# Projecting the small columns (decay, beta, forget gate) ahead of q, k and v in a hybrid mixer layer

## Chip, cores and metric

The kernel runs on one core of one Trainium2 chip. The metric is the device time of one execution in microseconds. The median of three runs of the kernel before is 900.4 us (899.67 to 903.23).

## What is computed

One transformer layer for a sequence of 512 tokens with 1024 channels, all in float32. The input is normalised to `h`, multiplied by one wide matrix `w_in`, and its columns feed four branches of 256 channels: a gated delta rule over chunks of 64 tokens, a latent attention, a gated linear attention and an attention with a forget gate. The branches are merged with sigmoid gates, and an MLP follows. The part that matters here is the delta rule's input and the rows of small columns:

```python
qkv = silu(causal_depthwise_conv(dn_qkv, dn_conv))          # 768 columns, 4 taps
a_q, a_k = l2_normalize(a_q), l2_normalize(a_k)             # per head of 64
beta = sigmoid(dn_b)                                        # 4 columns
g = -exp(dn_a_log) * softplus(dn_a + dn_dt_bias)            # 4 columns, cumsum per chunk
log_f = log_sigmoid(fox_f + fox_f_bias)                     # 4 columns, cumsum over the sequence
```

The sums of `g` become the decay factors of the delta rule, and the sums of `log_f` enter the logits of the forget-gate attention.

## The kernel before

**Matmuls.** Every float32 operand of a projection is split into a high part (a cast on ACT, L155) and a low part (a subtraction on DVE, L156), and a product is three matmuls (`mm3`, L250). `proj` (L254) computes 128 columns of a projection for all 512 tokens: 8 blocks of the 1024 channels, three matmuls each, 24 in all, into one accumulator in PSUM. The accumulators (`acc`) have two buffers.

**Weights.** `raw_cols` (L223) loads 128 columns of weights with a DMA on SP's queue into one of four raw buffers. `w_split` (L229) splits them into a pair of buffers, of which there are three.

**Order of the work.** The code is written in the order of the computation, and the framework then lays down one fixed queue per engine before the run, by the place in the program and by its own estimate of when inputs are ready. So later work fills gaps in earlier work, and an engine's queue need not follow the lines.

**Around the change.** After the input is normalised and the value columns of two branches are projected (L360 to L369), the loop of L396 projects q, k and v of the delta rule in six tiles of 128 columns (two each). For each tile DVE reads the accumulator four times (L399 and three times L402: the four taps of the convolution), `silu` (L371) takes three ACT steps and one DVE multiplication (L377), and the q and k tiles are squared, split and summed per head with matmuls (`sumsq`, L205, its matmuls L210 and L211) into `ps_n`. That is issued two tiles late, for m from 2 to 5.

Then comes a seventh tile, the small columns (`w_misc`, L413 and L414), whose columns the host has gathered. Rows 96 to 107 hold the forget gate, the decay and beta. DVE adds the bias (L420), ACT copies the other rows (L422), and POOL issues a load of a mask (L424). `softplus` (L379 to L392) is three ACT steps and seven DVE operations on 32 partitions. DVE scales (L429), scans along the tokens into RF (L430), clears a part (L431) and subtracts from the chunk's last sum (L433).

The tile RF then also gets the norms, in rows 0 to 31: a logarithm on ACT of `ps_n` (L436) and a DVE operation (L437). RS holds RF in two parts (L439 to L442). Matmuls with RF (L447) and RS (L456, L467) spread the rows for the decay matrices (`decay_pair`, L463); their results, times the products of keys and queries (L481, L485), go into the triangular solve. The projections of the gates and of the other branches (L529 to L580) fill TensorE meanwhile. Two DMAs per head on SP's queue (L546, L547) copy rows of RF for the forget-gate attention.

Temporaries (`tmp`) have four buffers; `softplus` takes three of them, `silu` one, `sumsq` three.

Of the kernel before, what the change touches and what calls it, by code (L numbers as in the profile page):

```python
# [12 lines left out]
ALU = mybir.AluOpType  # L13
# [3 lines left out]
P = 128  # L17
D = 1024
S = 512
# [17 lines left out]
DN_Q, DN_Z, DN_B, DN_A = 0, 768, 1024, 1028  # L37
# [16 lines left out]
V_CONV, V_PRE, V_MLP, V_BG, V_QN, V_KN, V_GB, V_DN, V_GN = 0, 24, 32, 40, 72, 74, 75, 76, 77  # L54
# [66 lines left out]
def hybrid_mixer_kernel(ctx, tc, I, out):  # L121
    nc = tc.nc
    pe, dve, act, pool, sp = nc.tensor, nc.vector, nc.scalar, nc.gpsimd, nc.sync
# [13 lines left out]
    def ps_acc():  # L137
        return psp.tile([P, 512], F32, name="acc", tag="acc", bufs=2)
# [3 lines left out]
    def ps_sm(*tags):  # L142
        tags = tags or banks["ring"]
        banks["i"] += 1
        t = tags[banks["i"] % len(tags)]
        return psp.tile([P, 512], F32, name=t, tag=t, bufs=1)
# [7 lines left out]
    def split(hi, lo, src, eng=dve):  # L154
        act.copy(out=hi, in_=src)  # L155
        eng.tensor_tensor(out=lo, in0=src, in1=hi.bitcast(F32), op=ALU.subtract)  # L156
# [37 lines left out]
    indz = const.tile([P, 134], F32R, name="indz")  # L194
# [10 lines left out]
    def sumsq(ps, lhsT, src, t, first, last):  # L205

        sq, hi, lo = t("sq"), t("sqh", F32R), t("sql", F32R)
        act.activation(out=sq, in_=src, func=AF.Square)
        split(hi, lo, sq)
        pe.matmul(out=ps, lhsT=lhsT, rhs=hi, start=first, stop=False)  # L210
        pe.matmul(out=ps, lhsT=lhsT, rhs=lo, start=False, stop=last)  # L211

    vec = lambda r: vecs[:, r:r + 1]
# [4 lines left out]
    w_in = I["w_in"][0]  # L218
# [4 lines left out]
    def raw_cols(w, c0):  # L223

        rv = raw_tile().rearrange("p (k c) -> p k c", k=KD)
        sp.dma_start(out=rv, in_=w.rearrange("(k p) c -> p k c", p=P)[:, :, c0:c0 + P])
        return rv

    def w_split(rv, where=None, eng=dve):  # L229
        wp, wb, tag = where or (wpool, 3, "w")  # L230
        hi = wp.tile([P, 1024], F32R, name="whi", tag=tag + "hi", bufs=wb)
        lo = wp.tile([P, 1024], F32R, name="wlo", tag=tag + "lo", bufs=wb)
        shape = rv.shape
        n = 1
        for d in shape[1:]:
            n *= d
        if len(shape) == 3:
            hv = hi[:, 0:n].rearrange("p (k c) -> p k c", k=shape[1])
            lv = lo[:, 0:n].rearrange("p (k c) -> p k c", k=shape[1])
        else:  # L240
            hv, lv = hi[:, 0:n], lo[:, 0:n]
        split(hv, lv, rv, eng)
        return hv, lv

    def stat_tiles(w, c0, ncol):

        for c in range(c0, c0 + ncol, P):
            yield w_split(raw_cols(w, c))
# [5 lines left out]
    def proj(wt, rh, rl, sl=slice(0, S), ps=None, clear=True):  # L254
        ps = ps_acc() if ps is None else ps
        hi, lo = wt
        for k in range(KD):
            mm3(ps[:, sl], hi[:, k], lo[:, k], rh[:, k, sl], rl[:, k, sl], clear and k == 0, k == KD - 1)
        return ps


    hh = big_tile("hh", F32R)
    hl = big_tile("hl", F32R)
# [81 lines left out]
    def slot(name, tag, bufs, dt=F32):  # L345
        return br.tile([P, S], dt, name=name, tag=tag, bufs=bufs)
# [14 lines left out]
    for g in range(2):  # L361
        ws = gv_w if g == 0 else [w_split(rows_4k(X_V, a)) for a in range(2)]
        for t in range(NT):
            ps = ps_acc()
# [6 lines left out]
    def silu(dst, src):  # L371

        sg = tmp("sg")
        act.activation(out=sg, in_=src, func=AF.Exp, scale=-1.0)
        act.activation(out=sg, in_=sg, func=AF.Ln, bias=1.0)
        act.activation(out=sg, in_=sg, func=AF.Exp, scale=-1.0)
        dve.tensor_tensor(out=dst, in0=src, in1=sg, op=ALU.mult)  # L377
# [14 lines left out]
        dve.scalar_tensor_tensor(out=dst, in0=z, scalar=0.0, in1=l, op0=ALU.max, op1=ALU.add)  # L392


    qkvT = []
    for m, wt in enumerate(stat_tiles(w_in, DN_Q, 768)):  # L396
        ps = proj(wt, hh, hl)
        y = slot("qkvT", "qkvT", 6)
        dve.tensor_scalar(out=y, in0=ps, scalar1=vec(V_CONV + 18 + m), scalar2=None, op0=ALU.mult)  # L399
        for j in range(3):  # L400
            sh = 3 - j
            dve.scalar_tensor_tensor(out=y[:, sh:], in0=ps[:, 0:S - sh], scalar=vec(V_CONV + 6 * j + m),  # L402
                                     in1=y[:, sh:], op0=ALU.mult, op1=ALU.add)
        silu(y, y)
        qkvT.append(y)
        if 2 <= m < 6:
            n_ = m - 2
            if n_ == 0:
                ps_n = ps_sm()
            sumsq(ps_n, indz[:, 6 - 2 * n_:6 - 2 * n_ + P], qkvT[n_], tmp, n_ == 0, n_ == 3)  # L410


    mraw = raw_cols(I["w_misc"], 0)  # L413
    misc = proj(w_split(mraw), hh, hl)  # L414
# [6 lines left out]
                      scalar2=cst[R9, _CO["rowc"][0]:_CO["rowc"][0] + 1], op0=ALU.add, op1=ALU.mult)  # L421
# [10 lines left out]
    gch = RF[R9].rearrange("p (n c) -> p n c", c=C)  # L432
    dve.tensor_tensor(out=RF[32:64].rearrange("p (n c) -> p n c", c=C),  # L433
                      in0=gch[:, :, C - 1:C].broadcast_to([32, NCH, C]), in1=gch, op=ALU.subtract)
    ps = ps_n
    act.activation(out=RF[0:32], in_=ps[0:32], func=AF.Ln, bias=eps_col[0:32])  # L436
    dve.tensor_scalar(out=RF[0:32], in0=RF[0:32], scalar1=-0.5,  # L437
                      scalar2=cst[0:32, _CO["rowc"][0] + 1:_CO["rowc"][0] + 2], op0=ALU.mult, op1=ALU.add)
# [6 lines left out]
    ps = ps_sm()  # L445
# [8 lines left out]
    ps = ps_sm()  # L454
# [52 lines left out]
    for p in range(2):  # L507
        ps = ps_sm()
# [8 lines left out]
    for src, outs in ((kbg, ((kbg, 4), (ktl, 12))), (vb, ((vb, 8),))):  # L517
        for p in range(2):
            ps = ps_sm()
            for j in range(NT):  # L520
                pe.transpose(out=ps[:, j * P:(j + 1) * P], in_=src[p][:, j * P:(j + 1) * P], identity=ident)
            for lst, c0 in outs:
                dve.tensor_tensor(
                    out=lst[p].rearrange("p (j e c) -> p j e c", j=NT, e=2),
                    in0=ps.rearrange("p (j e c) -> p j e c", j=NT, e=2),
                    in1=cols[:, :, c0 + 2 * p:c0 + 2 * p + 2].unsqueeze(3).broadcast_to([P, NT, 2, C]),
# [21 lines left out]
    for p in range(2):  # L548
        for c0, dst, sc in ((X_Q, fq, 0.125), (X_K, fk, 1.0)):
            ps = proj(w_split(raw_cols(w_in, c0 + P * p)), hh, hl)  # L550
# [3 lines left out]
    for wt in stat_tiles(w_in, G_Q, 256):  # L554
        ps = proj(wt, hh, hl)
# [3 lines left out]
    for wt in stat_tiles(w_in, M_CQ, 384):  # L559
        ps = proj(wt, hh, hl)  # L560
# [35 lines left out]
    for c in range(31, 0, -1):  # L596
# [4 lines left out]
                          in1=z0[:, c:c + 1, l_:16].broadcast_to([P, c, w_]), op=ALU.mult)  # L601
# [12 lines left out]
    for z in (1, 0):  # L614
        (pool, dve)[z].tensor_tensor(out=XD[z].rearrange("p g (b c) -> p g b c", c=32),
                           in0=XC[z].unsqueeze(2).broadcast_to([P, H * NT, 2, 32]),
                           in1=cv("blk2").unsqueeze(1).unsqueeze(3).broadcast_to([P, H * NT, 2, 32]), op=ALU.mult)
# [25 lines left out]
    for h in range(H):  # L643
        y = AT[h]
# [3 lines left out]
        ps = ps_sm()  # L648
# [7 lines left out]
        ps = ps_sm()  # L656
# [23 lines left out]
    for n in range(NCH):  # L680
        j, o = n // 2, n % 2
# [15 lines left out]
        if n < NCH - 1:  # L697
# [4 lines left out]
            for e in range(2):  # L702
                es = slice(C * e, C * e + C)
                for p in range(2):
                    dve.scalar_tensor_tensor(out=nxt[es, p, es], in0=cur[es, p, es], scalar=cd[es, p, n:n + 1],
                                             in1=psk[es, p * P + C * e:p * P + C * e + C], op0=ALU.mult, op1=ALU.add)
# [35 lines left out]
    ps = ps_sm()  # L742
# [5 lines left out]
    for n in range(NCH):  # L748
        cs = slice(C * n, C * n + C)
        dve.tensor_tensor_scan(out=gB[:, cs], data0=onesr.bitcast(F32)[:, 0:C], data1=gz[:, cs], initial=0.0,  # L750
                               op0=ALU.mult, op1=ALU.add)
# [9 lines left out]
                      in1=gBv[:, :, C - 1:C].broadcast_to([P, NCH, C]), op=ALU.subtract)  # L761
# [6 lines left out]
    ps = ps_sm()  # L768
# [58 lines left out]
    for h in range(H):  # L827
# [3 lines left out]
        ps = ps_sm()  # L831
# [13 lines left out]
    for n in range(NCH):  # L845
        j, o = n // 2, n % 2
# [8 lines left out]
        if n > 0:  # L855
            sm_ = gp.tile([P, 256], F32, name="Smask", tag="Smask", bufs=2)
            dve.tensor_tensor(out=sm_.rearrange("p (h c) -> p h c", c=C), in0=cur.unsqueeze(1).broadcast_to([P, H, C]),
                              in1=cv("bd32").rearrange("p (h c) -> p h c", c=C), op=ALU.mult)
# [3 lines left out]
        if n < NCH - 1:  # L862
# [7 lines left out]
            else:  # L870
                dve.scalar_tensor_tensor(out=nxt, in0=cur, scalar=cdg[:, n:n + 1], in1=psk[:, 0:C],
                                         op0=ALU.mult, op1=ALU.add)
# [54 lines left out]
    for p in range(2):  # L927
        ps = q_up(P * p)
# [3 lines left out]
    ps = q_up(256)  # L932
    dve.tensor_tensor(out=pe_c, in0=ps, in1=cs_sn[0], op=ALU.mult)
    pe_s = mt_("pe_s", "probT1", 2)
    ps = q_up(384)
# [8 lines left out]
    for p in range(2):  # L944
        ps = ps_sm()
# [5 lines left out]
    for t in range(NT):  # L951
        ps = ps_sm()
# [26 lines left out]
    for m in range(KD):  # L979
# [4 lines left out]
        for i in range(4):  # L984
            ps = ps_sm()
# [176 lines left out]
```

## Time and profile before

| | |
|---|---|
| median of three runs | 900.4 us (899.67 to 903.23) |
| profiled execution, its own time | 898.88 us |
| span from its first to its last instruction | 897.1 us |
| TensorE matmul busy | 879.0 us, 98% of the span |
| VectorE (DVE) busy | 441.4 us, 49% |
| ScalarE (ACT) busy | 394.0 us, 44% |
| GpSimd (POOL) busy | 118.5 us, 13% |
| mean granted TensorE clock | 0.997 |

Times in the profile are microseconds from the start of the span. Lines such as L447 are lines of the kernel. PE is TensorE's matmul, PEld its weight load, SP the engine that issues most DMAs. Matmuls overlap in the pipeline, so what one costs in a stream is the distance from start to start, not its own duration. A granted clock of 1.00 is 2.4 GHz and 0.50 is 1.2 GHz. The bracket at the end of a row of the timeline tells how long the engine stood idle before it and what ended that.

### The profile page before, as it was taken

The page shows a single profiled execution, that of the slowest core. Times are in us where ns is not written, and L with a number is a line of the kernel's source. Part 1 is how long each engine was busy: PE and PEld are TensorE (multiplying, and loading weights), DVE is VectorE, ACT ScalarE, POOL GpSimd, SP SyncE. Part 2 cuts the span into 40 slices and gives each one's busy share as a digit, 9 for nine tenths or more (in the row PEclk, how much of TensorE's full clock was granted, in tenths as well). Part 3 has the DMA queues.
Part 4 walks back from the last instruction along what each step waited for, and adds up shares of the span by engine and source line. Part 5 has one row for each costly group of instructions (what it writes and reads, how often), then busy time and mean ns, then how long its engine had stood idle before and what let it go on. Part 6 is the DMA issues. An engine that isn't in the chain of part 4 may idle for free.

```text
span 897.1 us, 11163 instructions
## 1 busy us (share of the span) xinstructions
PE 879.0 (98%) x4407; PEld 720.4 (80%) x4407; DVE 441.4 (49%) x717; ACT 394.0 (44%) x683; POOL 118.5 (13%) x112
## 2 busy tenths in 40 slices
PE   7999999999999998999999999999999999999997
PEld 7987788987767776888888789888888888888885
DVE  6388897446776674444336466322222333333324
ACT  6346553416976855444553354322223332222222
POOL 3100110110000002222015101322222200000000
PEclk9999999999999999999999999999999999999999
DMA  8433254402211111333333813333333332333202
GB/s 263 111 90 94 62 110 117 95 24 71 59 48 49 47 48 51 113 95 94 94 94 94 259 47 93 95 97 99 104 100 95 118 117 95 94 94 98 91 1 94
DMA packets 123700, 83.30 MB, mean 93 GB/s; under 512 B 19489, under 2 KB 115761, under 8 KB 123649
## 3 DMA queue, kind: packets, MB, share of 16 engines
q1 hardware_dynamic: 117696, 77.03, 29.8%
q10 hardware_dynamic: 5696, 4.73, 1.8%
q0 software_dynamic: 256, 0.85, 0.3%
q8 instruction: 34, 0.56, 0.3%
q14 instruction: 18, 0.14, 0.1%
HBM read 79.69 MB, written 2.88 MB: 92 GB/s over the span
## 4 chain that ended last, share of the span: by engine, by line
PE 92%; DVE 3%; ACT 1%; DMA 1%; POOL 1%; issue 1%; ACTq 0%; DVEq 0%; POOLq 0%
PE acc L252 56%; PE b L252 24%; PE b L790 2%; PE b L810 2%; PE b L284 1%; PE b L803 1%; DMA raw<-in_w_out_dram 1%; DVE wlo L156 1%; PE b L630 1%; PE b L834 1%; POOL gate L992 1%; PE b L481 0%; ACT whi L155 0%; PE b L659 0%; PE b L700 0%
## 5 line engine op out<-in xcount | busy, mean ns | idle before, releaser
L156 DVE TENSOR_TENSOR wlo<-raw,whi 128x1024 fp32r<-128x1024 f32 x134 | 172.1, 1287 | 258.7 <-ACT whi L155 257.9
L155 ACT CAST whi<-raw 128x1024 fp32r<-128x1024 f32 x136 | 142.3, 1049 | 272.2 <-PE acc L252 240.3
L252 PE MATMUL acc<-hh,whi 128*128 128x512 f32 x416 | 165.6, 398 | 0.1
L252 PE MATMUL acc<-hh,wlo 128*128 128x512 f32 x416 | 165.1, 397 | 0.0
L252 PE MATMUL acc<-hl,whi 128*128 128x512 f32 x416 | 164.1, 394 | 0.0
L252 PEld LDWEIGHTS acc<-hh,wlo 128*128 128x128 f32 x416 | 78.4, 189 | 17.1 <-issue 1.8
L252 PE MATMUL acc<-h2l,whi 128*128 128x512 f32 (+1 forms) x240 | 91.8, 382 | 0.0
L252 PE MATMUL acc<-h2h,whi 128*128 128x512 f32 (+1 forms) x240 | 91.7, 382 | 0.0
L252 PE MATMUL acc<-h2h,wlo 128*128 128x512 f32 (+1 forms) x240 | 91.7, 382 | 0.0
L252 PEld LDWEIGHTS acc<-hh,whi 128*128 128x128 f32 x416 | 78.5, 189 | 16.0 <-ACT gate L577 0.4
L252 PEld LDWEIGHTS acc<-hl,whi 128*128 128x128 f32 x416 | 78.3, 188 | 15.3 <-issue 0.3
L252 PE MATMUL b<-wlo,whi 128*128 128x512 f32 x192 | 74.7, 389 | 0.0
L252 PE MATMUL b<-whi 128*128 128x512 f32 x192 | 74.7, 389 | 0.0
L252 PE MATMUL b<-whi,wlo 128*128 128x512 f32 x192 | 74.7, 390 | 0.0
L252 PEld LDWEIGHTS acc<-h2h,wlo 128*128 128x128 f32 x240 | 45.1, 188 | 8.8
L252 PEld LDWEIGHTS acc<-h2l,whi 128*128 128x128 f32 x240 | 45.1, 188 | 8.8
L252 PEld LDWEIGHTS acc<-h2h,whi 128*128 128x128 f32 x240 | 45.1, 188 | 8.6
L992 POOL TENSOR_TENSOR gate<-gate 128x512 f32<-128x512 f32 x16 | 21.6, 1353 | 187.8 <-DVE gate L990 187.8
L252 PEld LDWEIGHTS b<-whi,wlo 128*128 128x128 f32 x192 | 36.0, 188 | 7.8 <-DVE wlo L156 0.4
L252 PEld LDWEIGHTS b<-wlo,whi 128*128 128x128 f32 x192 | 36.0, 188 | 7.6
L252 PEld LDWEIGHTS b<-whi 128*128 128x128 f32 x192 | 36.0, 188 | 7.5
L1068 POOL TENSOR_TENSOR u<-u 128x512 f32<-128x512 f32 x16 | 25.6, 1601 | 110.3 <-ACT u L1067 110.2
(315 smaller groups left out, 1407.4 us busy)
## 6 DMA issues: line engine op xcount, KB each, us to landing
raw<-in_w_gate_dram SPq DMA_DIRECT2D x32, 512.0 KB, 3.9
raw<-in_w_mlp_in_dram SPq DMA_DIRECT2D x32, 512.0 KB, 4.2
raw<-in_w_mlp_out_dram SPq DMA_DIRECT2D x32, 512.0 KB, 3.5
raw<-in_w_in_dram SPq DMA_DIRECT2D x23, 512.0 KB, 3.8
raw<-in_w_branch_up_dram SPq DMA_DIRECT2D x8, 512.0 KB, 3.9
raw<-in_w_out_dram SPq DMA_DIRECT2D x8, 512.0 KB, 3.6
x_t<-in_x_dram SPq DMA_DIRECT2D x4, 512.0 KB, 7.0
x<-in_x_dram ACTq DMA_DIRECT2D x1, 2048.0 KB, 12.1
```

Of the source, the lines that this page charges most:

```text
L155: act.copy(out=hi, in_=src)
L156: eng.tensor_tensor(out=lo, in0=src, in1=hi.bitcast(F32), op=ALU.subtract)
L252: pe.matmul(out=ps, lhsT=a, rhs=b, start=first and i == 0, stop=last and i == 2, skip_group_check=True)
L284: pe.transpose(out=ps[:, k * P:(k + 1) * P], in_=(src if late else sq)[:, ks], identity=ident)
L630: pe.matmul(out=pv[:, j], lhsT=av[h][:, j], rhs=src[:, j], start=j == 0, stop=j == NT - 1, skip_group_check=True)
L790: pe.matmul(out=ps[:, 0:n], lhsT=qT[e][0:rows, j * P:n], rhs=kT[e][0:rows, 0:n], start=True, stop=True)
L803: pe.transpose(out=pst[:, k * P:(k + 1) * P], in_=pr[:, k * P:(k + 1) * P], identity=ident)
L810: pe.matmul(out=psb[C * e:C * e + C, 0:P], lhsT=vt(k, 2 * p + e), rhs=pts[e][:, k * P:(k + 1) * P], start=k == 0, stop=k == j)
L834: pe.matmul(out=ps[:, js], lhsT=k_in[hs, js], rhs=q_in[hs, js], start=j == 0, stop=j == NT - 1, skip_group_check=True, tile_position=(32 * ...
L992: pool.tensor_tensor(out=g, in0=g, in1=gts[4 * m + i - 1], op=ALU.add)
L1068: pool.tensor_tensor(out=dst, in0=dst, in1=dst, op=ALU.mult)
```

## The change

The block of the small columns, from `mraw = raw_cols(...)` to the subtraction of L433, is moved as it is from behind the q, k and v loop to a place ahead of it. Nothing is added and nothing removed: the same instructions are issued, with other places in the program. The lines of the norms (L435 and after) stay where they are.

```diff
+    mraw = raw_cols(I["w_misc"], 0)
+    misc = proj(w_split(mraw), hh, hl)
+    RF = slot("RF", "rows", 2)
+    RS = slot("RS", "rows", 2, F32R)
...
+    softplus(zrow, zrow, R9)
+    dve.tensor_scalar(out=zrow, in0=zrow, scalar1=rowb[R9], scalar2=None, op0=ALU.mult)
+    dve.tensor_tensor_scan(out=RF[R9], data0=dmask[R9], data1=zrow, initial=0.0, op0=ALU.mult, op1=ALU.add)
+    dve.memset(RF[64:96], 0.0)
+    gch = RF[R9].rearrange("p (n c) -> p n c", c=C)
+    dve.tensor_tensor(out=RF[32:64].rearrange("p (n c) -> p n c", c=C),
+                      in0=gch[:, :, C - 1:C].broadcast_to([32, NCH, C]), in1=gch, op=ALU.subtract)
     qkvT = []
     for m, wt in enumerate(stat_tiles(w_in, DN_Q, 768)):
         ps = proj(wt, hh, hl)
...
             sumsq(ps_n, indz[:, 6 - 2 * n_:6 - 2 * n_ + P], qkvT[n_], tmp, n_ == 0, n_ == 3)
-
-    mraw = raw_cols(I["w_misc"], 0)
-    misc = proj(w_split(mraw), hh, hl)
...
-    dve.tensor_tensor(out=RF[32:64].rearrange("p (n c) -> p n c", c=C),
-                      in0=gch[:, :, C - 1:C].broadcast_to([32, NCH, C]), in1=gch, op=ALU.subtract)
     ps = ps_n
     act.activation(out=RF[0:32], in_=ps[0:32], func=AF.Ln, bias=eps_col[0:32])
```

## Rows read from the trace of the kernel before

**Rows 1.** The page, part 1: busy us (share of span) x instructions.

```profile
PE 879.0 (98%) x4407; PEld 720.4 (80%) x4407; DVE 441.4 (49%) x717; ACT 394.0 (44%) x683; POOL 118.5 (13%) x112
```

**Rows 2.** Waits of TensorE: waiting line, releaser: us in total, times, longest us.

```profile
PE b L252 <- ACT prob L798: 1.7, 1, 1.7
PE b L447 <- DVE RF L433: 1.7, 1, 1.7
...
PE b L252 <- ACT brh L155: 1.0, 1, 1.0
```

**Rows 3.** Chain that ended last, around L447: start us, us, what.

```profile
91.99 1.22 DVE RF L430
...
93.96 0.70 DVE RF L433
...
94.70 1.06 PE b L447 x8
```

**Rows 4.** Windows: PE, PEld, DVE, ACT, POOL busy (x), granted clock, DMA share, GB/s.

```profile
96.00:97.00 1.00, 1.00 (x5) 0.90 (x4) 0.99 (x1) 0.48 (x4) 0.00 (x0) 0.51 0.02 2
...
98.00:99.00 1.00, 1.00 (x4) 0.81 (x3) 0.36 (x2) 0.30 (x1) 0.00 (x0) 0.50 0.47 87
99.00:100.00 1.00, 1.00 (x5) 0.81 (x4) 1.00 (x5) 0.30 (x1) 0.00 (x0) 0.78 1.13 340
340.00:345.00 5.00, 3.30 (x17) 2.01 (x16) 2.07 (x6) 2.22 (x5) 0.00 (x0) 1.00 0.36 105
```

**Rows 5.** Timeline of TensorE, one tile's matmuls: start us, us, line, operation.

```profile
40.84 0.40 PE L252 MATMUL acc<-hh,whi 128*128 128x512 f32 x1
...
46.06 0.39 PE L252 MATMUL acc<-hh,wlo 128*128 128x512 f32 x1
```

**Rows 6.** Timeline of SP and POOL: the moved block's two loads.

```profile
42.95 0.37 SPq L226 DMA_DIRECT2D raw<-in_w_misc_dram  x1
...
26.52 0.56 POOL L424 DMA_DIRECT2D dmask<-in_cst_dram  x1
```

**Rows 7.** DMA issues by line: KB each, median us to landing.

```profile
raw<-in_w_misc_dram SPq DMA_DIRECT2D x1, 512.0 KB, 4.0
```

**Rows 8.** Timeline of ACT and DVE: the norms into RF.

```profile
82.31 0.68 ACT L436 ACTIVATE RF<-b,eps_col 32x512 f32<-32x512 f32 x1
...
83.03 0.47 DVE L437 TENSOR_SCALAR RF<-RF,cst 32x512 f32<-32x512 f32 x1 [0.80 <-ACT RF L436]
```

**Rows 9.** Timeline of DVE: first q tile's convolution, one split, one silu.

```profile
45.81 0.75 DVE L399 TENSOR_SCALAR qkvT<-acc,vecs 128x512 f32<-128x512 f32 x1 [2.89 <-PE acc L252]
...
47.26 1.21 DVE L156 TENSOR_TENSOR wlo<-raw,whi 128x1024 fp32r<-128x1024 f32 x1
48.39 1.53 DVE L402 SCALAR_TENSOR_TENSOR qkvT<-acc,vecs,qkvT 128x510 f32<-128x510 f32 x2
...
53.83 0.68 DVE L377 TENSOR_TENSOR qkvT<-qkvT,sg 128x512 f32<-128x512 f32 x1
```

**Rows 10.** Timeline of DVE: the block that is moved.

```profile
80.08 0.82 DVE L420 TENSOR_SCALAR zrow<-acc,vecs,cst 32x512 f32<-32x512 f32 x1 [0.64 <-PE acc L252]
...
86.00 0.69 DVE L387 TENSOR_TENSOR sp_m<-sp_m,sp_e 32x512 f32<-32x512 f32 x1
...
88.25 0.42 DVE L390 TENSOR_SCALAR sp_e<-sp_e 32x512 f32<-32x512 f32 x1
88.70 0.76 DVE L391 COPY_PREDICATED sp_l<-sp_e,sp_m 32x512 f32<-32x512 int32 x1
...
91.47 0.49 DVE L429 TENSOR_SCALAR zrow<-zrow,rowb 32x512 f32<-32x512 f32 x1
```

**Rows 11.** Timeline of ACT: a silu's wait, a split, one softplus step.

```profile
55.99 0.63 ACT L374 ACTIVATE sg<-qkvT 128x512 f32<-128x512 f32 x1 [3.27 <-DVE qkvT L402]
56.53 1.04 ACT L155 CAST whi<-raw 128x1024 fp32r<-128x1024 f32 x1
...
81.66 0.63 ACT L382 ACTIVATE sp_e<-zrow 32x512 f32<-32x512 f32 x1
```

More of the change, by code (lines that the diff above doesn't have):

```diff
@@ L392, in softplus @@
         dve.scalar_tensor_tensor(out=dst, in0=z, scalar=0.0, in1=l, op0=ALU.max, op1=ALU.add)
[L395 to L410, printed above, removed]
     mraw = raw_cols(I["w_misc"], 0)
@@ L434, in hybrid_mixer_kernel @@
                       in0=gch[:, :, C - 1:C].broadcast_to([32, NCH, C]), in1=gch, op=ALU.subtract)
+    qkvT = []
+    for m, wt in enumerate(stat_tiles(w_in, DN_Q, 768)):
+        ps = proj(wt, hh, hl)
+        y = slot("qkvT", "qkvT", 6)
+        dve.tensor_scalar(out=y, in0=ps, scalar1=vec(V_CONV + 18 + m), scalar2=None, op0=ALU.mult)
+        for j in range(3):
+            sh = 3 - j
+            dve.scalar_tensor_tensor(out=y[:, sh:], in0=ps[:, 0:S - sh], scalar=vec(V_CONV + 6 * j + m),
+                                     in1=y[:, sh:], op0=ALU.mult, op1=ALU.add)
+        silu(y, y)
+        qkvT.append(y)
+        if 2 <= m < 6:
+            n_ = m - 2
+            if n_ == 0:
+                ps_n = ps_sm()
+            sumsq(ps_n, indz[:, 6 - 2 * n_:6 - 2 * n_ + P], qkvT[n_], tmp, n_ == 0, n_ == 3)
     ps = ps_n
```

## Prediction

> **What bounds the kernel now.** I read the page's first part, then TensorE's waits, then the chain of waits, then windows. TensorE is busy for 98% of the span [rows 1], and the change moves its matmuls without adding or removing one. So only its waits, and stretches at half clock, can change the time. In the list of TensorE's waits [rows 2] most entries lie at the start, in the attention or at the load of the output weights. One belongs to the moved block: 1.7 us before L447, released by DVE's L433. The chain of waits around it [rows 3] shows why: L430, the scan, starts at 91.99 us and ends at 93.2, L433 at 94.66, and L447 starts at 94.70. The block is projected last of seven tiles, so the chain softplus, scan, L433 is late, and L447 needs all of RF.
>
> The wait costs more than itself. Behind it the granted clock is 0.51, 0.50 and 0.78 in three of the four windows from 96 to 100 us [rows 4] (97 to 98 is like 98 to 99): the lower level, 1.2 GHz. Lost matmul time is the sum of one minus the clock: 0.49 + 0.50 + 0.50 + 0.22 = 1.7 us. A wait of like length in the attention left the clock at 1.00: 340 to 345 us lost 5.00 - 3.30 = 1.7 us and stayed at full clock [rows 4].
>
> **The change part by part.** The sum is made against the profiled execution: 898.88 us, span 897.1, 1.5 us under the median of 900.4.
>
> *The projection moves.* Its 24 matmuls come before those of q, k and v. Between the first and the last of [rows 5] lie 23 starts in 5.22 us, so 0.227 each and 5.45 us per tile. All of it is work on the path in both places: 0. Its raw tile, loaded at 42.95 us as the seventh [rows 6], now goes ahead of the six q, k and v loads on SP, and each load then stands where another of 512 KB stood. The cover is the lead: 42.95 us against a projection that began about 74.6 (L420 at 80.08 [rows 10], less one tile). So 0; with the lead gone, 4.0 us of load [rows 7] and the split's 1.05 on ACT [rows 11] and 1.21 on DVE [rows 9], 6.3 us. POOL issues the mask load at 26.52 us [rows 6], behind eight memsets, far ahead of a scan that would now come at about 55; moving it past them costs POOL nothing. POOL's clearing of z0 (L593), which waited for the scan, comes earlier and gates nothing. Two row loads on SP that read RF (L546) can also go earlier.
>
> *The wait before L447 goes: minus 3.4 us.* Rows 96 to 127 of RF are then ready some 35 us earlier. What is late next is RF[0:32], the norms: L436 began at 82.31 and L437 ended at 83.5 us [rows 8]. Both move later by one tile, 5.45 us, to about 89, since the last key tile is projected one tile later. The order planned for TensorE was on time for the short chains of squares (the list of waits has no entry for L210 or L211) and 1.7 us too early over the long chain, so I take the wait as gone: 1.7 + 1.7 = 3.4 us. From below: nothing, if the short chain is late by as much. From above: 3.4 us plus a little, since the decay work begins some 5 us earlier.
>
> *A new wait on the convolutions: plus 1.5 us.* An accumulator has two buffers, so tile n's must be read out before tile n+2 starts: 5.45 us after tile n ends. Reading one out takes DVE four operations (L399 and three L402), and the trace [rows 9] shows them from 45.81 to 49.9 us, with a weight split (1.21 us) between them. So 4.1 of the 5.45 us are already used. Now put the moved block in front. It is all DVE's, on 32 partitions, at the price of 128 (L387 0.69 us, L377 0.68 [rows 9, 10]): L420 0.82; L386 and L390 0.42 each; L387 to L389 and L392 0.69 each; L391 0.76; L429 0.49 [rows 10]; then L430 1.22 and L433 0.70 [rows 3]. The sum is 0.82 + 0.84 + 2.76 + 0.76 + 0.49 + 1.22 + 0.70 = 7.6 us. The block's tile ends where q's first tile ended, at about 45.8. L420 ends at 46.6; two ACT steps of 0.63 us [rows 11] hold the chain until 47.9, and one weight split fits in there. By 51.25, when q's first tile is done, five of the operations are through (0.42 + 3 x 0.69 + 0.42 = 2.9) and L391 runs to 51.57. Two chains, each waiting for itself, then take turns: 4 x 0.75 for the convolution, L392, L429 and L430 between, ending at 51.57 + 3.0 + 2.4 = 57.0. The deadline is 45.8 + 2 x 5.45 = 56.7. With the next weight split among them, as in [rows 9], it is 58.2. So TensorE waits 0.3 us by the first count and 1.5 by the second; if L433 comes first too, 2.2. I take 1.5, since the rows show a split in that place in each tile. Lower bound 0 (the convolution goes first); upper bound 2.2, and 3.9 if half clock follows. Behind the convolution stand silu, the sums of squares and the later weight splits. Splits run almost two tiles ahead (the one at 47.26 is for a tile that starts near 57), so they absorb 2 us; one wait moves all later tiles and need not come again.
>
> ACT's part (four operations near 0.6 us, 2.5 in all) lies where it waited 3.27 us in the tile for DVE [rows 11]: 0; without that idle time, 2.5 us. The buffers of L381 hold three of four temporaries until about 54, and the first silu needs one: 0.
>
> The sum: 898.9 - 3.4 + 1.5 = 897.0, and 1.5 more on the scale of the median: **898.5 us**.
>
> The Trainium skill ("TensorE: Matmul & The Clock Gate", Part 1: The HAM clock gate) says that the throttled state is the default and that activity releases it, which speaks against any change that trades one wait for another. By it alone, the new wait could carry 1.7 us of half clock, and the sum would be 900.2. The window from 340 us, with as long a wait and a clock of 1.00 [rows 4], does not show that for every wait.
>
> **The rivals.** *No new wait* (0.16): the convolution goes ahead of the chain, 898.9 - 3.4 = 895.5, or 897.0 on the median's scale. The turn-taking in [rows 9] speaks against it.
>
> *The wait stays* (0.20): L447 waits as long for the norms, or the framework's own order has the block late as before: 900.4. With the new wait too, 901.9. For it: L437 is one more DVE operation in a stage where DVE hardly rests, and RF needs it.
>
> *DVE becomes the bound of this stage* (0.14; slower). Place: the read-outs from 56 to 80 us. A tile costs DVE 3.0 (read-out) + 1.21 (split) + 0.68 (L377) + 0.69 (the split of a square) = 5.6 of 5.45 us, plus some 0.7 us of waiting for the tile (as L420's 0.64 [rows 10]). If DVE can't start a read-out at once, the block's 7.6 us are not absorbed: 2.2 for the first tile and 0.15 + 0.7 for each of four more, so 5.6; with two stretches of half clock, 3.4 more. Against 3.4 saved: +5.6, or 906.0. It decides once the weight splits have used up their two tiles of lead.
>
> *More than the wait* (0.10; faster): the decays, the triangular solve and their output come 5 us earlier, and more gate projections are left as filler for the attention, where TensorE waits 1.7 and 1.0 us [rows 2]. If both go as well and no new wait comes: 3.4 + 2.7 = 6.1, so 894.3. Against it: those waits lie 250 us later, behind a softmax chain that the change doesn't touch.
>
> **How the numbers follow.** My forecast has 0.40, the others as given; 0.5% (4.5 us) is about what a measurement of this kernel can tell from no change. Faster than that is the last rival, 0.10; slower is DVE as bound, 0.14; the other three make 0.76. Range 894.0 to 905.5: it takes in every case within the bounds of the terms, reaches to the fast rival, and leaves out the worse half of DVE as bound and what a lost cover would cost.
>
> **What would show it.** TensorE's wait for L433 should be missing and the windows near 90 to 100 us at clock 1.00; the scan should start near 54 us instead of 91.99, and L447 near 90. TensorE should show a wait of 0.3 to 2.2 us near 57 us for L402. Wrong would be: L447 waiting for L437 or L440 for over 1 us; waits for L402 at several tiles; half clock behind the new wait; a wait at the first raw tile; or a difference that arises after 300 us.

## The result: slower by 0.6%, and the profile after

The kernel after takes 906.25 us (median of five runs, 905.9 to 906.57) against 900.25 us for the kernel before in the same job (899.67 to 903.23): a ratio of 1.0057, 95% interval 1.0038 to 1.0075. The prediction said 898.5 us and no change that can be measured. Its sign was wrong, and the time lies outside its range.

The profiled execution took 906.25 us, span 904.5. It is 7.4 us longer than the profiled execution before (898.88 us), which lay 1.4 us under its median; the medians are 6.0 us apart. Part 1 of the page of the kernel after:

```profile
PE 880.9 (97%) x4407; PEld 721.2 (80%) x4407; DVE 440.8 (49%) x717; ACT 394.5 (44%) x683; POOL 117.5 (13%) x112
```

The work is the same as in [rows 1], so again only waits and half clock can have changed. The waits of TensorE of the kernel after (line, releaser: us in total, times, longest):

```profile
PE acc L252 <- DVE qkvT L425: 3.8, 2, 3.5
PE b L284 <- DMA cst<-in_cst_dram: 2.2, 1, 2.2
...
PE acc L252 <- ACT fk L552: 1.7, 1, 1.7
```

Against [rows 2], the entry of L447 is gone, and the two of the attention and the output weights are what they were (1.7 and 1.0 us). Three are new or longer by over 1 us: 3.8 us for the read-out of the accumulators (L425 is L402 of before: three of the four taps; L422 is L399, the first), 1.7 us for fk, and 2.2 us at the start, where the list of before has 0.2.

Where is the time lost? The solve's matmuls (L630) serve as a marker. The timeline of TensorE, kernel before, and then kernel after:

```profile
165.69 3.68 PE L630 MATMUL b<-XD,ATs 128*128 128x64 f32 x32
```

```profile
173.44 3.68 PE L630 MATMUL b<-XD,ATs 128*128 128x64 f32 x32
```

From there to the end of the span it is 731.4 us before (897.1 - 165.69) and 731.1 after (904.5 - 173.44). So all of the 7.4 us of span arises ahead of the solve, which starts 7.7 us later (173.44 - 165.69). The first of the seven tiles ended at 45.81 us before [rows 9] and at 48.54 after; these 2.7 us arise before any of the moved chain has run on DVE, most of them at the wait for the first constants (2.2 us for 0.2). That leaves 5.0 us. The waits and the clock give 4.0 of them: 3.8 + 1.7 (half clock, below) + 1.9 (fk, with 0.2 for the weight split behind it) new, 1.7 + 1.7 gone. One us stays unassigned.

Windows of the kernel after (PE, PEld, DVE, ACT, POOL busy, granted clock, DMA share, GB/s):

```profile
69.00:70.00 1.00, 1.00 (x3) 0.82 (x4) 1.00 (x2) 0.97 (x2) 0.00 (x0) 0.53 0.00 0
70.00:71.00 1.00, 1.00 (x4) 0.81 (x3) 1.00 (x2) 0.75 (x2) 0.00 (x0) 0.50 0.05 16
71.00:72.00 1.00, 1.00 (x4) 0.72 (x4) 1.00 (x3) 0.00 (x0) 0.00 (x0) 0.50 0.26 33
72.00:73.00 1.00, 1.00 (x5) 0.82 (x4) 0.51 (x1) 0.46 (x1) 0.00 (x0) 0.76 1.07 311
...
96.00:97.00 1.00, 1.00 (x6) 0.82 (x5) 1.00 (x2) 1.00 (x3) 0.00 (x0) 1.00 0.00 0
```

The half clock near L447 [rows 4] is gone, and one of the same worth stands at 69 to 73 us: 0.47 + 0.50 + 0.50 + 0.24 = 1.7 us. What comes ahead of it is in TensorE's timeline:

```profile
59.64 0.50 PE L252 MATMUL acc<-hh,whi 128*128 128x512 f32 x1 [0.26 <-DVE qkvT L425]
...
65.03 0.39 PE L252 MATMUL acc<-hh,wlo 128*128 128x512 f32 x1
68.94 0.66 PE L252 MATMUL acc<-hh,whi 128*128 128x512 f32 x1 [3.53 <-DVE qkvT L425]
```

The third tile, at 59.64, waits 0.26 us for the first to be read out. The fourth, at 68.94, waits 3.53 us for the second. DVE's timeline in that stretch shows why:

```profile
58.83 0.75 DVE L425 SCALAR_TENSOR_TENSOR qkvT<-acc,vecs,qkvT 128x511 f32<-128x511 f32 x1
59.62 1.22 DVE L413 TENSOR_TENSOR_SCAN RF<-dmask,zrow 32x512 f32<-32x512 f32 x1
60.87 1.23 DVE L156 TENSOR_TENSOR wlo<-raw,whi 128x1024 fp32r<-128x1024 f32 x1
62.12 0.69 DVE L416 TENSOR_TENSOR RF<-RF 32x512 f32<-32x512 f32 x1
62.84 0.75 DVE L422 TENSOR_SCALAR qkvT<-acc,vecs 128x512 f32<-128x512 f32 x1
63.51 1.21 DVE L156 TENSOR_TENSOR wlo<-raw,whi 128x1024 fp32r<-128x1024 f32 x1
64.64 0.68 DVE L377 TENSOR_TENSOR qkvT<-qkvT,sg 128x512 f32<-128x512 f32 x1
65.25 0.74 DVE L425 SCALAR_TENSOR_TENSOR qkvT<-acc,vecs,qkvT 128x509 f32<-128x509 f32 x1
66.02 0.69 DVE L442 TENSOR_TENSOR RS<-RF,RS 32x512 fp32r<-32x512 f32 x1
66.73 0.75 DVE L425 SCALAR_TENSOR_TENSOR qkvT<-acc,vecs,qkvT 128x510 f32<-128x510 f32 x1
67.40 0.74 DVE L422 TENSOR_SCALAR qkvT<-acc,vecs 128x512 f32<-128x512 f32 x1
68.06 1.40 DVE L425 SCALAR_TENSOR_TENSOR qkvT<-acc,vecs,qkvT 128x511 f32<-128x511 f32 x2
```

The second tile's matmuls are through at about 59.4 us. Its first tap runs at 62.84, behind the scan (L413), a weight split and L416; its last at 68.06, behind another split, a product of silu (L377), L442, and the third tile's first tap (67.40). DVE stands still nowhere in this stretch, and each operation takes as long as before (0.75 for a tap, 1.21 for a split): there is only too much of it ahead of the one read that TensorE needs.

### The profile page after: what moved, and what is told of

Read it like the earlier page. It is cut to its first block, busy times and chain, and to the rows that moved or that the text cites. A ratio compares the mean times of both kernels' runs of the same rounds, so it can differ in the third digit from the quotient of the medians.

```text
span 904.5 us, 11163 instructions
## 1 busy us (share of the span) xinstructions
PE 880.9 (97%) x4407; PEld 721.2 (80%) x4407; DVE 440.8 (49%) x717; ACT 394.5 (44%) x683; POOL 117.5 (13%) x112
## 4 chain that ended last, share of the span: by engine, by line
PE 91%; DVE 4%; DMA 2%; ACT 1%; POOL 1%; issue 1%; ACTq 0%; DVEq 0%; POOLq 0%
PE acc L252 55%; PE b L252 24%; PE b L790 2%; PE b L810 2%; PE b L284 1%; PE b L803 1%; DVE wlo L156 1%; DMA raw<-in_w_out_dram 1%; PE b L630 1%; DMA cst<-in_cst_dram 1%; PE b L834 1%; POOL gate L992 1%; PE b L481 1%; DVE qkvT L425 0%; PE b L659 0%
## 5 line engine op out<-in xcount | busy, mean ns | idle before, releaser
L156 DVE TENSOR_TENSOR wlo<-raw,whi 128x1024 fp32r<-128x1024 f32 x134 | 172.0, 1287 | 258.7 <-ACT whi L155 258.0
```

## The experiments

The theory: the moved block and what follows from it fill DVE's queue while the first tiles have to be read out; the read-out of the second comes late by 3.5 us, and half clock follows. The rivals: the start (the loads) or the projection's new place does it, or ACT. Each run below is given with its own comparison against the kernel before on the same chip.

**The kernel before, unchanged.** 

> The kernel before, unchanged, for a second trace of its start. The changed kernel's first q, k or v split ran 2.7 us later than before, and TensorE's wait for the first constants was 2.2 us in place of 0.2. Theory 'start is chance': here that first wait comes out anywhere between 0.2 and 2.2 us with the same program. Theory 'start is the change': it is 0.2 us again, and every kernel with the block in front has about 2.2.

It took 899.64 us, with the wait before L447 (1.7 us) and the half clock behind it in place. They stand in both traces of this program.

**Six accumulators in place of two, on each kernel.** The loop's projections take their accumulator from the six PSUM buffers of the ring, so that a late read-out holds up nothing:

```diff
-        ps = proj(wt, hh, hl)
+        ps = proj(wt, hh, hl, ps=ps_sm())
```

> The changed kernel, but the six q, k and v projections accumulate in the six banks of the ring in place of the two accumulators. The order of DVE's queue stays the same. Theory 'read-out': TensorE's waits for L425 (0.4 and 3.7 us) and the half clock behind the long one (1.7 us) go, so 906.25 - 5.8 = 900.5 us; if more than that goes, the scan ahead of L447 no longer makes TensorE wait either and it is a little under 900. Theory 'knock-on or loads': the wait moves to another place and the time stays at 904 to 906 us.

> The kernel before with the same six banks, as a control. Its read-outs were in time, so both theories expect no change: 900 us, with the wait of 1.7 us before L447 and its half clock still there. If it is faster by over 2 us, the banks help by themselves and the run of the changed kernel with banks must be read against this one.

On the kernel after: 902.16 us, ratio 1.0014 (1.0002 to 1.0025). The wait on L425 and the half clock are gone, with 4.1 us. So the late read-outs are most of the cost. But two waits remain, the one on fk and a new one. TensorE's timeline in this run:

```profile
72.72 0.39 PE L252 MATMUL b<-hl,whi 128*128 128x512 f32 x1
74.44 0.50 PE L210 MATMUL b<-sqh,indz 128*128 128x512 f32 x1 [1.33 <-ACT sqh L155]
```

The squares of the first tile are late now: the same delay, handed on to the next that reads it. On the kernel before: 900.96 us, ratio 1.0007 (0.9994 to 1.0021), the wait before L447 1.0 us with no half clock behind it.

**Only the projection moved.** On the kernel before, L413 to L424 (projection, L420, L422, mask load) go in front of the loop, and softplus and the scan stay behind it:

```diff
+    misc = proj(w_split(mraw), hh, hl)
...
     for m, wt in enumerate(stat_tiles(w_in, DN_Q, 768)):
...
-    misc = proj(w_split(mraw), hh, hl)
...
     softplus(zrow, zrow, R9)
```

> The changed kernel, but only the projection and its two read-outs (L403, L405 of the changed kernel) stand in front; softplus, scan and the subtraction are back behind the q, k and v loop. Theory 'read-out': DVE's chain in front is what makes the read-outs late, so no wait for L425's kin, and the old wait for the scan before L447 is back: 900 to 902 us. Theory 'the moved projection or its load costs': still 904 to 906 us.

901.64 us, ratio 1.0006 (0.999 to 1.0022): no wait on a read-out, and the wait on L433 is still there with 1.9 us. So neither the place of the matmuls and loads nor the two read-outs of that tile is the cost; the chain of softplus and scan is, and it is the gain as well.

**A shorter chain.** On the kernel after, softplus leaves out its polynomial (L386 to L391, six DVE operations of 3.7 us) for the small columns:

```diff
+        if rows != slice(96, 128):
-        dve.tensor_scalar(out=m, in0=e, scalar1=-0.25, scalar2=1.0 / 3.0, op0=ALU.mult, op1=ALU.add)
+            dve.tensor_scalar(out=m, in0=e, scalar1=-0.25, scalar2=1.0 / 3.0, op0=ALU.mult, op1=ALU.add)
...
-        dve.copy_predicated(out=l, mask=e.bitcast(I32), data=m)
+            dve.copy_predicated(out=l, mask=e.bitcast(I32), data=m)
```

> The changed kernel without softplus' polynomial for small exponentials on the small columns (L386 to L391): six of DVE's operations, 0.42 + 3 x 0.69 + 0.42 + 0.76 = 3.7 us, are left out; nothing else moves. Theory 'read-out': the waits for L425 (0.4 and 3.7 us) and the half clock go: 906.25 - 5.8 = 900.5 us, the wait of 1.7 us for fk's read-out on ACT stays. Rival 'the place of the projection, its load or the start': DVE's 3.7 us less change nothing: 905 to 906 us.

901.48 us, ratio 1.0009 (0.9998 to 1.002). With 3.7 us less in DVE's queue the wait on the taps falls from 3.5 to 0.7 us and the half clock goes. The fk entry is gone too; in its place stands a wait of 1.4 us on a weight's low part at 118 us.

**The taps first.** On the kernel after, the four taps get priority over the rest in the framework's order:

```diff
+        with tc.high_priority():
             dve.tensor_scalar(out=y, in0=ps, scalar1=vec(V_CONV + 18 + m), scalar2=None, op0=ALU.mult)
...
```

> The changed kernel with the four read-outs of each q, k and v tile at high priority for the framework, which puts L416, L442 and the third tile's first read-out behind parts of the second tile's read-outs; nothing is added or left out. Theory 'read-out': 0.69 to 1.4 us of other work less stands ahead of the second tile's last read-out, so the long wait is 2.3 to 3.0 us in place of 3.7; 904 to 905.5 us with the half clock, 903 without. Rival: 906 us.

903.01 us, ratio 1.0024 (1.0016 to 1.0033). No instruction is left out, only the order is another, and the wait falls from 3.8 to 2.3 us in two with the clock at 1.00; in the place of the fk entry stands 1.5 us on a weight's low part. So part of the wait is order, and the rest is what stands ahead of the taps in any order.

**The low parts of the weights on POOL.** On the kernel after, the splits of the loop's weights (L156) leave DVE:

```diff
-    for m, wt in enumerate(stat_tiles(w_in, DN_Q, 768)):
+    for m, wt in enumerate(stat_tiles(w_in, DN_Q, 768, pool)):
...
```

> The changed kernel with the low parts of the six q, k and v weight tiles made on POOL (about 2.4 us each there) in place of DVE (1.2 us each). The moved block stays whole. Theory 'read-out': DVE has 1.2 us per tile more, 3.6 us by the second tile's deadline, so the long wait shrinks from 3.7 us to about 0.5 and its half clock goes: 901 us. Rival: 905 to 906 us, or later if POOL's longer splits make TensorE wait.

907.32 us, ratio 1.007 (1.0056 to 1.0084): a miss, though DVE issues two operations of 1.2 us less in the stretch. The wait on L425 is 3.1 us in two. POOL's timeline in this run, and then DVE's:

```profile
54.51 2.38 POOL L156 TENSOR_TENSOR wlo<-raw,whi 128x1024 fp32r<-128x1024 f32 x1 [3.09 <-ACT whi L155]
...
64.70 2.40 POOL L156 TENSOR_TENSOR wlo<-raw,whi 128x1024 fp32r<-128x1024 f32 x1 [1.45 <-issue]
```

```profile
54.44 0.75 DVE L422 TENSOR_SCALAR qkvT<-acc,vecs 128x512 f32<-128x512 f32 x1
55.22 2.28 DVE L391 COPY_PREDICATED sp_l<-sp_e,sp_m 32x512 f32<-32x512 int32 x1
...
65.24 2.41 DVE L377 TENSOR_TENSOR qkvT<-qkvT,sg 128x512 f32<-128x512 f32 x1
```

L391 takes 2.28 us where it took 0.76 [rows 10], and L377 2.41 where it took 0.68. POOL's splits end at 56.89 and 67.10 us, L391 and L377 at 57.50 and 67.65: each about one duration of its own behind POOL. The tap at 54.44, which reads PSUM, keeps its 0.75 while POOL begins. So the move to POOL gains nothing here: for each split of 1.2 us that left its queue in these rows, DVE loses 1.5 or 1.7 us at another operation. The Trainium skill ("SBUF — State Buffer", Who interferes with whom) says that a DVE instruction with two SBUF inputs contends with a GpSimd instruction that reads SBUF, for a port pair that one of them holds alone; these rows agree. Half clock adds to this run's time: it stands at the 2.2 us wait (clock 0.50 from 61 to 64 us) and behind the 1.7 us wait on fk (0.50 from 126 to 129).

**The block in the middle.** The whole block stands ahead of the fourth of the six tiles (`if m == 3:` in the loop). 

> The block stands ahead of the fourth of the six q, k and v tiles in place of the first. Theory 'read-out': DVE has no more room there (it also splits the squares), so the same 7.6 us make the read-outs of the fifth and sixth tile late: a wait of 2 to 4 us for them some 16 us later than in the changed kernel, 903 to 906 us. Rival 'only the front is a bad place': no wait for read-outs, the scan still in time for L447, 897 to 899 us, faster than both.

908.43 us, ratio 1.008 (1.0061 to 1.01), the slowest of all. The waits on taps are small (0.6 us on L425's counterpart), but the squares (L210, L211) wait 1.5 us each, a weight split 1.7, and half clock lies from 85 to 92 us. The backlog costs in this place too, and the waits have other names.

**The first tap on ACT, with two and with six accumulators, on each kernel.**

```diff
-        dve.tensor_scalar(out=y, in0=ps, scalar1=vec(V_CONV + 18 + m), scalar2=None, op0=ALU.mult)
+        act.activation(out=y, in_=ps, func=AF.Copy, scale=vec(V_CONV + 18 + m))
```

> The kernel after, with the first tap of the convolution (L422, the scaled read of the accumulator) on ACT instead of DVE; nothing else. Theory (the second q tile's read-outs come late because DVE has the rest of the small columns' block, a silu product, a split and the third tile's taps ahead of them, all about 0.7 us each): one DVE operation less per tile, two of them ahead of the second tile's last tap, so the wait of 3.5 us at L425 falls to 2 us or less, the half clock behind it goes too, time 902 to 904 us. Rival (the second tile's tap is held by the scan itself, a block that doesn't split): the wait stays above 3 us with its half clock, time 905 to 907.

> The kernel before with the same move of the first tap to ACT: the control. Theory: no convolution waits here, so nothing goes there; the wait of 1.7 us before L447 and the half clock behind it shrink only as far as DVE's queue ahead of the small columns' block becomes shorter: 898 to 901 us. Rival (TensorE loses elsewhere whenever ACT takes 0.7 us more per tile): over 902.

> The kernel after with the first tap on ACT and the projections of the loop in the six PSUM buffers of the ring: both reliefs at once. Theory: no wait on a convolution, no half clock at 69 us, and the squares' matmuls (L210), which waited 1.5 us with the six buffers alone, wait under 0.7 us because DVE and the taps run ahead: 900 to 901.5 us, no better than before, since the wait of ACT's queue at 122 us (1.7 us on fk) and the longer start are not touched. Rival (with two accumulators more the gain before L447 shows in full): under 899.

> The kernel before with both reliefs, the control for the run with both on the kernel after. Theory: the wait before L447 is under 1 us as with the six buffers alone (1.0), time 899 to 901 us, so that after with both is the same as this within 1 us. Rival (the moved block is worth 3.4 us once nothing waits on read-outs): after with both is 2 us or more below this one.

On the kernel after: 904.69 us, 1.0049 (1.0033 to 1.0066). The longest wait is 2.1 us, down from 3.5 as the theory has it, but half clock still follows. On the kernel before: 902.73 us, 1.0024 (1.001 to 1.0039), over what I expected, so the tap on ACT has a price of its own. With six accumulators: 901.78 us, 1.0014 (1.0002 to 1.0025), on the kernel after, 901.08, 1.0008 (0.9995 to 1.0021), on the kernel before. The squares still wait (1.3 us in two), against the theory.

**What became of the 3.4 us.** With the read-outs free, the kernel after is still not below the kernel before with the same edit. The stall at 122 us is the suspect. Timelines of the kernel after, of TensorE, ACT and DVE:

```profile
122.03 0.39 PE L252 MATMUL acc<-hh,whi 128*128 128x512 f32 x1
122.26 0.39 PE L252 MATMUL acc<-hl,whi 128*128 128x512 f32 x1
124.33 0.50 PE L252 MATMUL acc<-hh,whi 128*128 128x512 f32 x1 [1.68 <-ACT fk L552]
...
125.25 0.50 PE L252 MATMUL acc<-hh,wlo 128*128 128x512 f32 x1 [0.20 <-DVE wlo L156]
...
130.15 0.62 PE L252 MATMUL acc<-hh,wlo 128*128 128x512 f32 x2
```

```profile
122.00 1.05 ACT L155 CAST whi<-raw 128x1024 fp32r<-128x1024 f32 x1 [0.52 <-PE acc L252]
123.08 1.20 ACT L552 ACTIVATE fk<-acc 64x512 f32<-64x512 f32 x2
```

```profile
123.98 3.50 DVE L156 TENSOR_TENSOR wlo<-raw,whi 128x1024 fp32r<-128x1024 f32 x3
```

TensorE begins a tile at 122.03, but its third matmul does not follow 122.26: the low part that it reads is not made yet. The framework's fixed queue puts another tile in between, 24 matmuls from 124.33 on, and takes the first tile up again behind it, which is why two matmuls with a low part follow each other at 130.15. The tile in between needs the other of the two accumulators, the one that the fk copies read, and starts 0.05 us after they end (124.28). The copies stand on ACT behind a weight cast that itself waited for TensorE. DVE's low parts begin only at 123.98, three that have piled up. Windows of DVE's busiest stretch, kernel before and then kernel after:

```profile
110.00:120.00 10.00, 9.93 (x56) 8.03 (x53) 9.97 (x21) 7.46 (x13) 6.06 (x4) 1.00 0.43 41
```

```profile
110.00:120.00 10.00, 10.00 (x69) 7.97 (x66) 9.96 (x25) 7.47 (x16) 5.95 (x4) 1.00 0.58 67
```

DVE is busy for 9.97 of 10 us in one and 9.96 in the other. First the copies alone got priority:

```diff
+            with tc.high_priority():
                 for e in range(2):
                     act.activation(out=dst[2 * p + e][0:C], in_=ps[C * e:C * e + C], func=AF.Copy, scale=sc)
```

> The kernel after, with the copies of fq and fk out of the accumulators (L552, ACT) given priority over the work around them; nothing else. Theory (ACT's queue has the steps of silu and a weight cast that itself waits ahead of these copies; a second wait that belongs to the change): the 1.7 us wait on fk near 122 us goes, the convolution's 3.5 us and its half clock stay, time 903.5 to 905 us. Rival (ACT has too much there in any order, so the wait only changes its name): a wait of 1 us or more on whi, wlo or another read near 120 us, time 905.5 to 907.

> The kernel after with the six PSUM buffers for the loop and the priority of the fq and fk copies: both waits that came with the change are taken away. Theory (the 3.4 us before L447 are a real gain that these two waits ate): 898 to 900 us, 2 us or more below the kernel with the six buffers alone (902.16). Rival (what is saved before L447 is lost again wherever DVE or ACT is next late): no more than 0.7 us below it.

> The kernel before with the same two edits, the control. Theory: no fk wait here, so no more than the six buffers alone: 900 to 902 us, wait before L447 about 1.0 us, and the kernel after with both edits lies 1 to 3 us below this one. Rival: both within 0.7 us of each other, so the move is worth nothing even with its own waits taken away.

On the kernel after: 906.52 us, 1.006 (1.0045 to 1.0076), with the wait still there (1.6 us). The copies stand behind the same cast as before (cast at 121.79, copies at 122.74), so ACT's order there was not changed by it. With the six accumulators: 900.8 us, 1.0004 (0.9993 to 1.0015), on the kernel after, with the fk wait at 1.7 us, and 900.79, 1.0004 (0.9991 to 1.0016), on the kernel before. Then the splits of these weights got priority as well:

```diff
+            rv = raw_cols(w_in, c0 + P * p)
+            with tc.high_priority():
+                wt = w_split(rv)
+            ps = proj(wt, hh, hl)
-            ps = proj(w_split(raw_cols(w_in, c0 + P * p)), hh, hl)
```

> The kernel after with the six PSUM buffers, and priority both for the splits of the weights of fq and fk (L155 on ACT, L156 on DVE) and for their copies (L552). Theory (the stall near 118 us is DVE's: the low part of the next weights stands behind L523, L377 and L540 in a stretch where DVE is 99% busy, and the copies of fk end at the same moment): with the splits ahead of them the 1.7 us wait falls under 0.5 us; time 898.5 to 900.5 us. Rival (the work of DVE and ACT there is what bounds it, in any order): TensorE waits 1 us or more on another reader near 105 to 125 us, time 900.5 to 902.5.

> The kernel before with the same edits, the control. Theory: the wait before L447 stays at 1.0 us or so and nothing else changes, 900 to 901.5 us, so that the kernel after with these edits lies 1 to 2 us below. Rival: both within 0.7 us of each other.

> The kernel after with the two accumulators as they were, and priority for the splits and copies of fq and fk alone. Theory: the 3.5 us on the convolution and its half clock stay, the 1.7 us near 122 us goes: 903.5 to 905 us. Rival (the wait changes its name): 905.5 to 907 us.

Now the wait on fk is gone on both forms of the kernel after. ACT's timeline of the kernel after with these priorities:

```profile
122.96 1.20 ACT L556 ACTIVATE fk<-acc 64x512 f32<-64x512 f32 x2 [0.42 <-PE acc L252]
124.06 1.04 ACT L155 CAST whi<-raw 128x1024 fp32r<-128x1024 f32 x1
```

The copies come ahead of the cast, the next low part is made at 114.38, and TensorE works its tiles one after another. The list's name for the wait, the fk copies, is right: in all seven runs that list it, TensorE starts within 0.06 us of the end of the second copy, while the first low part begins 0.1 to 1.3 us ahead of that start. But the tile that waits for the copies stands there because another had no low part; with the taps first and with the shorter chain TensorE keeps its order and waits 1.5 and 1.4 us for that low part itself. Whether the earlier low part or the copies ahead of the cast counts for more isn't told apart, since the edit moves both. On the kernel after with two accumulators: 905.2 us, 1.0054 (1.0039 to 1.0069), only 1 us less than without the edit, since a half clock at 101 to 105 us takes 1.7 back. With six: 900.21 us, 0.9999 (0.9987 to 1.0011), on the kernel after, and 899.4, 0.9994 (0.9983 to 1.0005), on the kernel before. The largest waits that remain in the stretch in question, TensorE's timeline of the kernel after and of the kernel before with these edits:

```profile
73.91 0.50 PE L210 MATMUL b<-sqh,indz 128*128 128x512 f32 x1 [1.33 <-ACT sqh L155]
```

```profile
95.66 1.06 PE L447 MATMUL b<-cst,RF 128*128 128x16 f32 x8 [1.22 <-DVE RF L433]
```

One waits 1.33 us for the squares, the other 1.22 us for RF. That is the trade: block late, RF waits; block early, the convolutions and their squares wait.

The two runs of a row were compared with the same runs of the kernel before:

| edit | on before, us | on after, us |
|---|---|---|
| none | 900.25 | 906.25 |
| first tap on ACT | 902.73 | 904.69 |
| six accumulators | 900.96 | 902.16 |
| six, first tap on ACT | 901.08 | 901.78 |
| six, priority for fq and fk copies | 900.79 | 900.80 |
| six, priority for their splits and copies | 899.40 | 900.21 |

In no row is the kernel after ahead, and no version beats the kernel before by more than its interval.

## Why the prediction was wrong

**The projection, 0.** Right. TensorE waits for no weights at its new place, and the run that moved it alone measures no difference.

**The wait before L447, minus 3.4 us.** Right for the kernel as it is: the wait and the half clock are gone, and L447 (99.43 us) follows L437 (98.88) with no wait, though 9 us later than I thought, for what was lost ahead of it and at the start. The second half of the term was weaker than it looked. With the wait before L447 in place, half clock followed it in the kernel before (1.7 us), with the projection moved (1.9) and with six accumulators and the tap on ACT (1.4), and not with the tap on ACT alone (1.8). That 1.7 us was not bound to the wait. Nor did the attention's wait always leave the clock alone, as it did in [rows 4]: in the kernel after with six accumulators and the splits first it is as long (1.67 us), and half clock follows it; one of the windows:

```profile
345.00:346.00 1.00, 1.00 (x5) 0.90 (x4) 0.00 (x0) 0.43 (x1) 0.00 (x0) 0.50 1.07 324
```

The one window that the prediction read could not settle whether such a wait brings half clock.

**A new wait on the convolutions, plus 1.5 us.** This is the step that failed. For the first tile its first count was good, 0.3 us for 0.26 measured; the 1.5 us that it took was its second count, with a split among the taps, and that split ran only behind the taps and the scan (60.87 us). What failed is its last sentence, that one wait moves all later tiles "and need not come again": the wait came again at the second tile's read-out, with 3.5 us, so that the term came to 3.8 us and not 1.5. It held against the second tile nothing but its own taps. The rows show ahead of them what the step itself had listed for DVE but used only up to the first deadline: the scan, L416, two splits, the product of silu, and L442, which it had not listed. Six accumulators took away 4.1 of the 6.0 us, and a chain shorter by 3.7 us took 2.8 us off the wait. Half clock behind the new wait and waits at more than one tile were among the prediction's own signs of being wrong.

**Half clock behind it.** The step kept 3.9 us as the bound with half clock, and the sentence on the Trainium skill ("TensorE: Matmul & The Clock Gate", Part 1: The HAM clock gate), by which activity releases a throttle that is the default, gave 900.2 us. Half clock did follow the 3.5 us wait, worth 1.7 us, and there the trace agrees with the page. It did not follow the 1.7 us wait on fk in this kernel, though it did with the low parts on POOL.

**What is late next.** The prediction named the norms alone. Later on lies a stretch in which DVE is busy for over 99% of the time in both kernels. The splits did absorb part of the delay, as the prediction said, but with their lead: between the end of the first tile and this stretch DVE makes nine low parts of weights in the kernel before (47.26 to 96.01 us) and eight in the kernel after (49.40 to 97.74). Here the missing one is due, and TensorE waits 1.7 us, and 0.2 more for the low part itself. The terms ACT 0 and "absorb 2 us" were counted for the loop and not for this stretch.

**The start** (2.7 us in the profile) was in no term. The wait for the first constants is 2.2 us in the profile of the kernel after and 0.2 in both of the kernel before. But waits of TensorE of the kernel before with six accumulators, and then of the kernel after with priority for the fk copies, read:

```profile
PE b L284 <- DMA cst<-in_cst_dram: 2.5, 1, 2.5
```

```profile
PE b L284 <- DMA cst<-in_cst_dram: 0.3, 1, 0.3
```

The first of the seven tiles ends between 45.8 and 48.6 us in the kernels with the whole block in front, and between 45.8 and 48.4 in those with it behind; in the two traces of the unchanged kernel before, at 45.81 and 46.61. So the moved block is not its cause. What is, stays open. Of the 6.0 us between the medians the waits and the clock account for 4.0; the rest has no place in this account.

**The rivals.** The one that came true is that DVE becomes the bound of the stage, to which I gave 0.14: its place (the read-outs from 56 to 80 us) was right. Its price (plus 5.6, 906.0 us) came out near by luck: it was 5.6 us of waits on the taps and 3.4 of half clock, where 3.8 and 1.7 were measured and 1.9 came from fk. Its form was not right: one wait of 3.5 us on the second tile, and not some 0.85 us on each of several. Its count, DVE 5.6 of 5.45 us per tile, takes in a square's split, which the rows up to the long wait do not show; there a tile costs DVE 4.9. In the kernel before DVE rested 0.73, 0.73 and 0.64 us ahead of the third, fourth and fifth tile. Even so 7.6 us put in front cannot be absorbed at some 0.7 us per tile by the second tile's deadline, which was a reason to take this rival as the likeliest.

## What to carry to other kernels

When a chain is moved ahead of a loop, add up what the engine that runs it has to do per turn of the loop. If it has little to spare there, what the turns up to a buffer's next deadline cannot take up comes out as waits of the loop, at the second deadline as well as the first, and may come to more than the wait that is saved later. Follow the queue to the second and third user of each buffer, and count what is left of the lead of the work that is done ahead. And when the list names a wait after a copy, look at the order of the engine that waits: here it was in the middle of one tile and waited to begin another.

## What the runs showed of the hardware

**Equal waits, unequal clocks.** With the taps first, TensorE stood still from about 65.3 to 67.52 us; with the first tap on ACT, from about 56.5 to 58.76. Windows behind the wait, of the first of these kernels and then of the second:

```profile
68.00:69.00 1.00, 1.00 (x6) 0.78 (x6) 1.00 (x2) 0.94 (x3) 0.00 (x0) 1.00 0.85 229
```

```profile
59.00:60.00 1.00, 1.00 (x3) 0.81 (x4) 0.97 (x2) 1.00 (x3) 0.00 (x0) 0.50 0.04 4
```

The distances from start to start are 2.46 and 2.47 us, in both cases between full streams of 128x512 matmuls; one clock stays at 2.4 GHz, the other falls to 1.2.

**Half clock with no wait at all.** Timeline and windows of TensorE of the kernel after with priority for the splits and copies:

```profile
98.24 1.07 PE L447 MATMUL b<-cst,RF 128*128 128x16 f32 x8
99.24 0.93 PE L481 MATMUL b<-qkvT 64*128 64x128 f32 x10
100.29 0.39 PE L456 MATMUL b<-RS,selt 128*128 128x8 f32 x2
```

```profile
99.00:100.00 1.00, 1.00 (x13) 0.95 (x12) 0.62 (x2) 0.21 (x1) 0.00 (x0) 1.00 0.07 16
100.00:101.00 1.00, 0.88 (x6) 0.59 (x4) 0.23 (x1) 0.40 (x3) 0.00 (x0) 1.00 0.00 0
101.00:102.00 1.00, 1.00 (x4) 0.84 (x4) 0.06 (x1) 0.61 (x2) 0.00 (x0) 0.72 0.00 0
102.00:103.00 1.00, 1.00 (x4) 0.71 (x4) 0.96 (x4) 1.00 (x4) 0.00 (x0) 0.50 0.00 0
```

TensorE is busy for 1.00 and 0.88 of the two windows ahead of the fall, and its list of waits has no entry there; the matmuls are narrow (16, 128 and 8 columns), and the clock falls behind them. So here a group of narrow matmuls stood where elsewhere a wait did. That is not a rule either: in the kernel after the same lines run from 98.78 to 101.07 us (L481, L447, L481) and the clock stays at 1.00. Whether L447's own narrow matmuls had a part in the half clock of [rows 4] no run shows.
